# Grouped-query attention on one core: the values' cast moves from a GpSimd instruction to GpSimd's transfers, with a re-made plan of the work

## The chip, the cores and the metric

The kernel runs on one core of one Trainium2 chip. The metric is the device time of one execution in microseconds. A core has a matrix engine (PE in the profile, with its weight loads as PEld), a vector engine (DVE), a scalar engine (ACT), a general engine (POOL, also called GpSimd), and a queue engine (SP) that here only issues transfers. Each engine runs its own instructions in order; semaphores tie them to one another. Transfers (DMAs) can be issued by SP, by ACT and by POOL.

## The reference

Eight batches, eight query heads, two key and value heads, 1024 positions, head size 64, all in float32. Four query heads share one key and value head. For each of the 64 query heads the kernel must compute

```
scores = scale * matmul(q, k.T)          # 1024 x 1024, scale = 1 / 8
attn   = exp(scores - max(scores))
attn   = attn / (sum(attn) + 1e-08)
out    = matmul(attn, v)                 # 1024 x 64
```

## The kernel before, in words

**Jobs and pairs.** Each query head is a job j, 0 to 63 (NJ = 64). A job's scores are computed turned, keys on the partitions, as eight *pairs* of two 128x512 blocks. A pair fills one of three PSUM slots (`sp0` to `sp2`), written by two matmuls (L864), and it is then turned into exponentials in one of two ways.

**The ACT way.** One ACTIVATE over 128x1024 (L874) writes bf16 exponentials into a `pt` tile. PE multiplies them with the values: eight matmuls a pair.

**The DVE way.** One TENSOR_SCALAR, the *first pass* (L885, `dpass`), scales the scores and writes them as 16-bit integers into `yt`, which read as bf16 are nearly powers of two. Two pairs form a *chain*. Over a chain DVE runs two masking instructions on 2048 columns, `zh` (L892) for the mantissa part and `two` (L899) for the exponent part, and a product (L908, `mul`), in place in `zt`. Then PE adds both parts, `et` and `zt`, by matmuls of their own, sixteen a pair. Only for the last four jobs does DVE add them (L913).

**GpSimd's share.** Part of a chain's product is computed by GpSimd (L835, `gmul`), some columns at a time, each while DVE runs a first pass (and the normalization behind it, if there is one). Such a stretch is called a window. The planner works out how many columns fit a window from M_GFIX (fixed ns) and M_GCOL (ns a column), in steps of 32 columns and at least 192. A chain is given up to two windows before DVE does the rest, and only chains that begin with heads 2 to 58 take part.

**Values.** The values of a group (four jobs) stand in one of four `va` tiles of 128 x 4 x 2 x 65 bf16; the 65th number is 1, so the matmuls (L926) also sum the exponentials. SP loads them as float32 into `vs` (L656), and GpSimd casts them into `va` with one instruction (L659, `place_v`). For groups 1 to 15 the planner has an event of its own, `gplace` (L215 to L219): the cast takes 614 ns of a window, and a product follows in the same window only if at least 192 columns still fit.

**Queries and keys.** They are cast to bf16 by transfers that GpSimd issues, from DRAM to DRAM (L623 for one or two heads, L632 for the last head), and turned into SBUF by transposing transfers that SP issues (L667, L677). A cast is due 18 us (q) or 19 us (k) before its first scores and a transpose 11 or 12.5 us. Once GpSimd has had its first product, a cast that is due stands in a list (`casts`). It is issued behind a product when the next product's planned start leaves 650 ns (M_ISSUE, L843); if it gets 5 us late it is issued at once, behind the newest score matmul.

**Output.** A group of up to seven 128-row pieces is finished by a RECIPROCAL (L991, `rec`) and a multiplication (L1000, `norm`) on DVE, then stored by SP (L1004).

**The order.** All of this is laid out by `Plan` when the kernel is built. It steps through a model of PE, ACT and DVE with the M_ constants as durations. At each choice of PE (a score pair for ACT or DVE, a piece of the value matmuls, a dummy matmul, waiting) it looks HORIZON ns ahead, and takes the choice with the least idle time of ACT and DVE, weighted by W_A and W_D (and PE's waste by W_P). `quota` (L151) caps how many of a job's eight pairs go to DVE: FIRST for the first jobs, then MXD, and one more in each MORE-th job. M_BACK caps DVE's backlog when a pair is given to it, M_SPARE says how near the next first pass must be for DVE to leave a chain's product to GpSimd, M_HOLD how long a normalization may wait. The resulting list of events is the order in which each engine gets its instructions.

Of the kernel before, what the change touches and what calls it, by code (L numbers as in the profile page):

```python
# [17 lines left out]
M_FILL = 1e9  # L18
M_IDLE = 350
M_DUMMY = 110  # L20
# [16 lines left out]
M_GLEAD = 160  # L37
M_GFIX = 120
M_GCOL = 2.09
M_GOVER = 60  # L40
M_GLATE = 900
M_NORM = 531
M_HOLD = 2500
M_SPARE = 500
M_ISSUE = 650

M_GAP = 90
M_RUNWAY = 1800
M_BACK = 3000
M_WAIT = 250  # L50
M_TOL = 300

HORIZON = 5500
W_A = 1.0
W_D = .28
W_P = 0
W_LAG = 0
# [4 lines left out]
MXD = 2  # L62
MORE = 6
TAIL = 4
CHN = 2
LONG = 6
FIRST = (2, 1)
GWINS = 2
# [66 lines left out]
class Plan:  # L135
# [5 lines left out]
    def __init__(self, nj, npt, nct, nyt):  # L141
# [32 lines left out]
        s.firstp, s.fleft, s.twice = [INF] * 8, 8, []  # L174
        s.placed = 0
        s.end = False
# [31 lines left out]

    def gpsimd(self, s, t, j, window):

# [3 lines left out]
        at += M_GLEAD  # L214
        g = s.placed + 1  # L215
        if 4 * g - 1 <= j < self.nj and 4 * g < self.nj and at + 614 <= until:
            s.placed = g
            s.note(t, "gplace", None, g, None)
            at = s.tG = at + 614  # L219
        for ch in s.chains:  # L220
# [19 lines left out]
    def dve(self, s):  # L240
# [4 lines left out]
        if rec:  # L245
            _, _, lo, hi = s.norms[0]
            if soon:
                self.gpsimd(s, t, s.dq[0][2], M_REC + 1134 + M_NORM)
                s.host = True
# [4 lines left out]
        elif s.dq and s.dq[0][0] <= t and not (norm and t - s.norms[0][0] > M_HOLD):  # L254
# [15 lines left out]
            if not s.host:  # L270
                self.gpsimd(s, t, j, 1134 + (M_NORM if norm else 0))
            s.host = False
# [271 lines left out]
def kernel(  # L544
# [37 lines left out]
    qp = ctx.enter_context(tc.tile_pool(name="qp", bufs=8))  # L582
    vsp = ctx.enter_context(tc.tile_pool(name="vsp", bufs=2))
    pp = ctx.enter_context(tc.tile_pool(name="pp", bufs=NPT))
# [43 lines left out]
    def cast_q(j):  # L628
        b, h = divmod(j, H)
        if j == NJ - 1:  # L630
            t = qd[j] = dram.tile([HS, 2 * D], BF16, name=f"qd{j}")
            return nc.gpsimd.dma_start(  # L632
                out=t.rearrange("(c p) d -> p c d", p=128), in_=rows(q[b, h], True)
            )
        n = 2 if j > 2 else 1
        t = dram.tile([n * HS, 2 * D], BF16, name=f"qd{j}")
        for i in range(n):
            qd[j + i] = t[i * HS : (i + 1) * HS, :]
        return cast(q.rearrange("b h s d -> (b h s) d")[j * S : (j + n) * S, :], t)
# [13 lines left out]
    def load_v(b, g):  # L653
        t = vsp.tile([128, NH, 2 * D], FP32, name="vs")
        vs[(b, g)] = t
        return nc.sync.dma_start(out=t, in_=rows(v[b, g], b == g == 0))  # L656

    def place_v(b, g):
        return nc.gpsimd.tensor_copy(  # L659
            out=va[(b * G + g) % NVA][:, :, :, 0:D],  # L660
            in_=vs.pop((b, g)).rearrange("p c (two d) -> p c two d", two=2),
        )

# [16 lines left out]
    need, pvs, done = {}, {}, {}  # L680
    places = {}
    for t, kind, x, j, *_ in plan.ev:
        if kind == "score":
            need.setdefault(j, t)
        if kind == "pv":
            pvs.setdefault(x // NPIECE, t)
        if kind == "gplace":
            places[j] = t

# [72 lines left out]
    for j in range(NJ):  # L762
# [15 lines left out]
    for x in [e for e in plan.ev if e[1] == "norm"]:  # L778
# [28 lines left out]

    begun = [e for e in ev if e[1] in ("gmul", "gplace")]
    starts = [e[0] + M_GLEAD for e in begun] + [INF]
# [4 lines left out]
    def begin(kind, j, gate):  # L814
        ins = cast_k(*j) if kind == "ck" else cast_q(j)
        if now and gate:
            tc.add_manual_dep(ins.ins, now.ins.name, Sync, reason="loads in time, not sooner")

    for when, kind, x, j, c, *cols in ev:
        if casts and casts[0][0] < when - 5000:  # L820
            begin(*casts.pop(0)[1:], True)
        if kind in ("ck", "cq"):
# [5 lines left out]
        elif kind in ("gmul", "gplace"):  # L828

            if kind == "gplace":  # L830
                gps = place_v(*divmod(j, G))
            else:
                lo, w = c
                z = flat(zt[j])[:, lo : lo + w]
                gps = nc.gpsimd.tensor_tensor(  # L835
                    out=z, in0=flat(yt[j])[:, lo : lo + w], in1=z, op=ALU.mult
                )
# [12 lines left out]
        elif kind == "tq":  # L850
            turn_q(j)
        elif kind == "lv":
            load_v(*j)
        elif kind == "pl":
# [184 lines left out]
```

## Time and profile before

| | |
|---|---|
| median of 3 runs | 358.98 us (358.1 to 359.25) |
| the profiled execution | 358.87 us, its span 357.0 us |
| granted TensorE clock | 0.998 |
| busy: PE, DVE, ACT, POOL | 345.1, 347.9, 347.3, 149.8 us |
| first exponentials on ACT, last end on ACT | 6.19 us, 351.5 us |
| ACT exponentials (L874) | 374, 344.8 us busy |
| DVE first passes (L885) | 138, 167.6 us busy |
| GpSimd products (L835) | 98, 113.7 us busy |
| GpSimd casts of values (L659) | 16, 10.2 us busy |
| GpSimd issues of q and k casts (L623, L632) | 41, 27.2 us |
| DMA engines, mean share by queue | 41.9% (SP's), 19.3% (GpSimd's) |

The busy time of a group is the time in which at least one of its instructions ran; the mean duration beside it in the lines below is that of one instruction with its tail. Two DVE instructions in a row overlap by about 0.08 us, and ACT's by about 0.12 us, so the time from one start to the next is shorter than the mean. A POOL line with DMA_DIRECT2D is the time GpSimd takes to issue a transfer, not the time of the transfer.

### The profile page before, as it was taken

The page shows a single profiled execution, that of the slowest core. Times are in us where ns is not written, and L with a number is a line of the kernel's source. Part 1 is how long each engine was busy: PE and PEld are TensorE (multiplying, and loading weights), DVE is VectorE, ACT ScalarE, POOL GpSimd, SP SyncE. Part 2 cuts the span into 40 slices and gives each one's busy share as a digit, 9 for nine tenths or more (in the row PEclk, how much of TensorE's full clock was granted, in tenths as well). Part 3 has the DMA queues.
Part 4 walks back from the last instruction along what each step waited for, and adds up shares of the span by engine and source line. Part 5 has one row for each costly group of instructions (what it writes and reads, how often), then busy time and mean ns, then how long its engine had stood idle before and what let it go on. Part 6 is the DMA issues. An engine that isn't in the chain of part 4 may idle for free.

```text
span 357.0 us, 13990 instructions
## 1 busy us (share of the span) xinstructions
PE 345.1 (97%) x6196; PEld 221.2 (62%) x6196; DVE 347.9 (97%) x512; ACT 347.3 (97%) x378; POOL 149.8 (42%) x161
## 2 busy tenths in 40 slices
PE   7899999999999999999999999999999999999995
PEld 3456566666666666666666666666666666666764
DVE  5999999999999999999999999999999999999995
ACT  5999999999999999999999999999999999999993
POOL 3015465654547455345454445222464543531000
PEclk9999999999999999999999999999999999999999
DMA  7937748657646686478655775666854865734323
GB/s 176 118 76 120 150 93 190 146 98 161 137 105 106 157 140 148 80 146 166 121 119 130 126 150 125 130 131 107 146 133 99 161 155 101 147 83 87 77 62 120
DMA packets 88221, 44.82 MB, mean 126 GB/s; under 512 B 45408, under 2 KB 87008, under 8 KB 87520
## 3 DMA queue, kind: packets, MB, share of 16 engines
q1 hardware_dynamic: 86208, 33.44, 41.9%
q0 software_dynamic: 1808, 10.23, 19.3%
q8 instruction: 48, 0.79, 0.9%
q10 hardware_dynamic: 144, 0.26, 0.2%
q14 instruction: 13, 0.11, 0.1%
HBM read 25.17 MB, written 27.00 MB: 146 GB/s over the span
## 4 chain that ended last, share of the span: by engine, by line
ACT 49%; PE 28%; DVE 18%; DMA 2%; issue 2%; DVEq 0%; POOLq 0%
ACT pt L874 49%; PE ops L926 15%; PE sp L864 12%; DVE yt L885 9%; DVE zt L908 3%; DVE et L899 2%; DVE ost L1000 2%; DVE zt L892 1%; DMA qt<-qd 1%; DMA qd<-in_q_dram 1%; PE sp L966 1%; DVE rec L991 1%; DVEq L899 0%; POOLq L1023 0%
## 5 line engine op out<-in xcount | busy, mean ns | idle before, releaser
L874 ACT ACTIVATE pt<-sp 128x1024 bf16<-128x1024 f32 x374 | 344.8, 1041 | 0.8 <-PE sp L864 0.5
L864 PE MATMUL sp<-qt,kt 64*128 64x512 bf16 x1024 | 172.6, 382 | 5.7 <-DVE yt L885 1.6
L926 PE MATMUL ops<-va,pt 128*128 128x65 bf16 x2904 | 175.3, 194 | 0.0
L885 DVE TENSOR_SCALAR yt<-sp 128x1024 uint16<-128x1024 f32 x138 | 167.6, 1214 | 1.0 <-PE sp L864 1.0
L835 POOL TENSOR_TENSOR zt<-yt,zt 128x416 bf16<-128x416 bf16 (+3 forms) x98 | 113.7, 1160 | 111.3 <-DVE et L899 52.8
L926 PEld LDWEIGHTS <-pt 128*128 128x128 bf16 x2904 | 128.3, 97 | 32.5 <-issue 32.5
L926 PE MATMUL ops<-va,zt 128*128 128x65 bf16 x1064 | 126.1, 194 | 0.6 <-DVE zt L908 0.6
L926 PE MATMUL ops<-va,et 128*128 128x65 bf16 x1016 | 117.5, 194 | 0.0
L926 PEld LDWEIGHTS <-zt 128*128 128x128 bf16 x1064 | 84.9, 97 | 14.4 <-issue 13.5
L926 PEld LDWEIGHTS <-et 128*128 128x128 bf16 x1016 | 80.1, 98 | 21.7 <-issue 21.7
L864 PEld LDWEIGHTS <-kt 64*128 64x128 bf16 x1024 | 48.1, 93 | 56.4 <-issue 33.9
L908 DVE TENSOR_TENSOR zt<-yt,zt 128x960 bf16<-128x960 bf16 (+7 forms) x70 | 56.4, 807 | 0.0
L892 DVE TENSOR_SCALAR zt<-yt 128x2048 uint16<-128x2048 uint16 (+1 forms) x70 | 47.6, 680 | 0.3
L899 DVE TENSOR_SCALAR et<-yt 128x2048 uint16<-128x2048 uint16 (+1 forms) x70 | 46.7, 673 | 0.0
L1000 DVE TENSOR_TENSOR ost<-ops,rec 128x448 f32<-128x448 f32 (+2 forms) x73 | 44.3, 606 | 0.2
L623 POOL DMA_DIRECT2D qd<-in_q_dram x32 | 21.1, 658 | 20.2 <-PE sp L864 19.4
L659 POOL CAST va<-vs 128x512 bf16<-128x512 f32 x16 | 10.2, 635 | 34.0 <-DVE ost L1000 15.6
L991 DVE RECIPROCAL rec<-ops 128x7 f32<-128x7 f32 (+2 forms) x73 | 14.1, 194 | 0.0
L623 POOL DMA_DIRECT2D kd<-in_k_dram x8 | 5.3, 666 | 6.9 <-PE ops L926 4.9
L713 PE MATMUL ops<-warm 128*128 128x128 bf16 (+1 forms) x28 | 5.5, 318 | 1.2 <-DVE warm L617 1.2
L913 DVE TENSOR_TENSOR zt<-et,zt 128x2048 bf16<-128x2048 bf16 (+1 forms) x5 | 5.5, 1100 | 0.0
L713 PEld LDWEIGHTS <-warm 128*128 128x128 bf16 x28 | 2.3, 112 | 3.9 <-issue 2.8
(37 smaller groups left out, 23.4 us busy)
## 6 DMA issues: line engine op xcount, KB each, us to landing
out_dram<-ost SPq DMA_DIRECT2D x64, 256.0 KB, 3.2
qd<-in_q_dram POOLq DMA_DIRECT2D x30, 256.0 KB, 4.6
vs<-in_v_dram SPq DMA_DIRECT2D x16, 256.0 KB, 3.8
kt<-kt SPq DMA_DIRECT2D x30, 64.0 KB, 2.8
kd<-in_k_dram POOLq DMA_DIRECT2D x7, 256.0 KB, 5.0
qt<-qd SPq DMA_TRANSPOSE x63, 3.8
qd<-in_q_dram POOLq DMA_DIRECT2D x3, 128.0 KB, 4.0
q<-in_q_dram ACTq DMA_DIRECT2D x1, 256.0 KB, 3.4
```

The costliest lines, as they stand in the source:

```text
L623: return nc.gpsimd.dma_start(out=t.rearrange("(a x) d -> a (x d)", a=128), in_=src.rearrange("(a x) d -> a (x d)", a=128),)
L659: return nc.gpsimd.tensor_copy(out=va[(b * G + g) % NVA][:, :, :, 0:D], in_=vs.pop((b, g)).rearrange("p c (two d) -> p c two d", two=2),)
L835: gps = nc.gpsimd.tensor_tensor(out=z, in0=flat(yt[j])[:, lo : lo + w], in1=z, op=ALU.mult)
L864: now = nc.tensor.matmul(sps[x][:, half, :], lhsT=t[lo : lo + D, c // NH, ci % NH * 128 : (ci % NH + 1) * 128], rhs=qt[j][lo : lo + D, 0, ...
L874: exps.append(nc.scalar.activation(out=p, in_=where_s[(j, c)], func=AF.Exp, scale=scale))
L885: vec = nc.vector.tensor_scalar(out=yt[ch][:, i, :, :], in0=where_s[c], scalar1=EXP_A, scalar2=EXP_B, op0=ALU.mult, op1=ALU.add,)
L892: vec = nc.vector.tensor_scalar(out=zt[j][:, 0:c], in0=yt[j][:, 0:c], scalar1=0x7F, scalar2=0x3F00, op0=ALU.bitwise_and, op1=ALU.bitwise_or,)
L899: vec = ins = nc.vector.tensor_scalar(out=et[j][:, 0:c], in0=yt[j][:, 0:c], scalar1=0x7F80, scalar2=None, op0=ALU.bitwise_and,)
L908: vec = nc.vector.tensor_tensor(out=z, in0=flat(yt[j])[:, 0 : cols[0]], in1=z, op=ALU.mult)
L926: nc.tensor.matmul(ops[plan.group_of[x] % 2][:, lo : lo + D + 1], lhsT=p[:, qs * 128 : (qs + 1) * 128], rhs=va[(b * G + h // HPG) % NVA][: ...
L991: vec = nc.vector.reciprocal(out=to, in_=sums)
L1000: vec = nc.vector.tensor_tensor(out=to, in0=o, in1=by, op=ALU.mult)
```

## The change

Groups 1 to 15 of the values no longer go through `vs` and a GpSimd instruction. For each group two transfers issued by GpSimd read the float32 values in DRAM and write bf16 straight into `va`, one for the even and one for the odd rows of a pair (`two` = 0 and 1). They are due 12 us before the group's first scores and go through the same list as the other casts. The planner's `gplace` event is gone, and with it `placed`, `places` and the load by SP; group 0 is still loaded by SP and cast by GpSimd. Query casts are grouped otherwise: head 3 alone, heads 4 and 5, ..., 60 and 61 in twos, 62 and 63 alone; the first casts and transposes get due times just behind the first scores, where they were before them. The planner's constants change, and so its list of events.

```
-M_IDLE = 350
+M_IDLE = 250
-M_GFIX = 120
-M_GCOL = 2.09
+M_GFIX = 190
+M_GCOL = 1.88
-M_HOLD = 2500
-M_SPARE = 500
+M_HOLD = 1500
+M_SPARE = 800
-M_RUNWAY = 1800
-M_BACK = 3000
+M_RUNWAY = 2100
+M_BACK = 4100
-M_TOL = 300
-HORIZON = 5500
+M_TOL = 200
+HORIZON = 7000
-W_P = 0
+W_P = 0.02
-MORE = 6
+MORE = 4
-FIRST = (2, 1)
+FIRST = (2, 2, 1)
...
-        g = s.placed + 1
-        if 4 * g - 1 <= j < self.nj and 4 * g < self.nj and at + 614 <= until:
-            s.placed = g
-            s.note(t, "gplace", None, g, None)
-            at = s.tG = at + 614
...
-        n = 2 if j > 2 else 1
+        n = 2 if 3 < j < NJ - 2 else 1
...
+    def cast_v(b, g, two):
+        return nc.gpsimd.dma_start(
+            out=va[(b * G + g) % NVA][:, :, two, 0:D],
+            in_=v[b, g].rearrange("(c p two) d -> p c two d", p=128, two=2)[:, :, two, :],
+        )
...
-                ev.append((at - 19000, "ck", None, (b, g), None))
+                ev.append((max(at - 19000, M_START + 200), "ck", None, (b, g), None))
...
-            ev.append((places[j // HPG] - 8000, "lv", None, (b, g), None))
+            for two in range(2):
+                ev.append((at - 12000, "cv", None, (b, g, two), None))
...
-        if j > 2 and (j % 2 or j == NJ - 1):
-            ev.append((at - 18000, "cq", None, j, None))
+        if j == 3 or (j > 3 and j % 2 == 0) or j == NJ - 1:
+            ev.append((max(at - 18000, M_START + 100), "cq", None, j, None))
         if j > 1:
-            ev.append((at - 11000, "tq", None, j, None))
+            ev.append((max(at - 11000, M_START + 100 * j), "tq", None, j, None))
...
-            took = 614 if kind == "gplace" else M_GFIX + M_GCOL * c[1]
+            took = M_GFIX + M_GCOL * w
```

More of the change, by code (lines that the diff above doesn't have):

```diff
@@ L42 @@
 M_NORM = 531
-M_HOLD = 2500
-M_SPARE = 500
+M_HOLD = 1500
+M_SPARE = 800
 M_ISSUE = 650
 M_GAP = 90
-M_RUNWAY = 1800
-M_BACK = 3000
+M_RUNWAY = 2100
+M_BACK = 4100
 M_WAIT = 250
-M_TOL = 300
-HORIZON = 5500
+M_TOL = 200
+HORIZON = 7000
 W_A = 1.0
-W_D = .28
-W_P = 0
+W_D = 0.28
+W_P = 0.02
 W_LAG = 0
@@ L174, in __init__ @@
         s.firstp, s.fleft, s.twice = [INF] * 8, 8, []
-        s.placed = 0
         s.end = False
@@ L207, in act, with gpsimd @@
             self.ready(s, j, c, s.slot[sl])
-    def gpsimd(self, s, t, j, window):
+    def gpsimd(self, s, t, window):
         at = max(t, s.tG)
@@ L247, in dve @@
             if soon:
-                self.gpsimd(s, t, s.dq[0][2], M_REC + 1134 + M_NORM)
+                self.gpsimd(s, t, M_REC + 1134 + M_NORM)
                 s.host = True
@@ L270, in dve @@
             if not s.host:
-                self.gpsimd(s, t, j, 1134 + (M_NORM if norm else 0))
+                self.gpsimd(s, t, 1134 + (M_NORM if norm else 0))
             s.host = False
@@ L582 @@
     qp = ctx.enter_context(tc.tile_pool(name="qp", bufs=8))
-    vsp = ctx.enter_context(tc.tile_pool(name="vsp", bufs=2))
+    vsp = ctx.enter_context(tc.tile_pool(name="vsp", bufs=1))
     pp = ctx.enter_context(tc.tile_pool(name="pp", bufs=NPT))
@@ L655, in load_v @@
         vs[(b, g)] = t
-        return nc.sync.dma_start(out=t, in_=rows(v[b, g], b == g == 0))
+        return nc.sync.dma_start(out=t, in_=rows(v[b, g], True))
     def place_v(b, g):
@@ L680 @@
     need, pvs, done = {}, {}, {}
-    places = {}
     for t, kind, x, j, *_ in plan.ev:
@@ L686 @@
             pvs.setdefault(x // NPIECE, t)
-        if kind == "gplace":
-            places[j] = t
     f32 = {x: kvp.tile([128, NH, 2 * D], FP32, name=f"{x}32") for x in "kq"}
@@ L806, in terms @@
                 yield ci, pt[(j, c)][:, par, :]
-    begun = [e for e in ev if e[1] in ("gmul", "gplace")]
+    begun = [e for e in ev if e[1] == "gmul"]
     starts = [e[0] + M_GLEAD for e in begun] + [INF]
@@ L814, in begin @@
     def begin(kind, j, gate):
-        ins = cast_k(*j) if kind == "ck" else cast_q(j)
+        ins = cast_q(j) if kind == "cq" else (cast_k if kind == "ck" else cast_v)(*j)
         if now and gate:
@@ L821 @@
             begin(*casts.pop(0)[1:], True)
-        if kind in ("ck", "cq"):
+        if kind in ("ck", "cq", "cv"):
             if gps is None:
@@ L827 @@
                 casts.append((when, kind, j))
[L828 to L837, printed above, removed]
+        elif kind == "gmul":
+            lo, w = c
+            z = flat(zt[j])[:, lo : lo + w]
+            gps = nc.gpsimd.tensor_tensor(
+                out=z, in0=flat(yt[j])[:, lo : lo + w], in1=z, op=ALU.mult
+            )
             tc.add_manual_dep(gps.ins, vec.ins.name, Sync, reason="VectorE needs the port before")
-            took = 614 if kind == "gplace" else M_GFIX + M_GCOL * c[1]
+            took = M_GFIX + M_GCOL * w
             free = max(free, when + M_GLEAD) + took
@@ L851 @@
             turn_q(j)
-        elif kind == "lv":
-            load_v(*j)
         elif kind == "pl":
```

## The prediction

> **What bounds the kernel now.** I read the busy shares first, then the stretches, then the groups of instructions by form, then single passages of the timeline. The busy shares alone leave three candidates:
>
> ```profile
> PE 345.1 (97%) x6196; PEld 221.2 (62%) x6196; DVE 347.9 (97%) x512; ACT 347.3 (97%) x378; POOL 149.8 (42%) x161
> ```
>
> The stretches from the middle of the run (columns: us, then PE, PEld, DVE, ACT and POOL, each with its number of instructions, clock, DMA share, GB/s):
>
> ```profile
> 80.00:120.00 40.00, 39.84 (x730) 25.71 (x728) 40.00 (x62) 40.00 (x45) 21.92 (x22) 1.00 0.63 124
> 200.00:240.00 40.00, 39.82 (x733) 25.95 (x732) 39.93 (x58) 40.00 (x45) 15.59 (x17) 1.00 0.60 121
> 280.00:320.00 40.00, 39.77 (x716) 25.41 (x713) 39.90 (x58) 40.00 (x44) 18.09 (x18) 1.00 0.62 130
> ```
>
> DVE and ACT have no hole at all; the clock is full. PE's share is one of overlapping matmuls and is no bound. So the end moves only if both ACT and DVE get less to do. POOL has time, but only between and beside DVE's instructions. The groups by form give the prices:
>
> ```profile
> L874 ACT ACTIVATE pt<-sp 128x1024 bf16<-128x1024 f32 x374 | 344.8, 1041 | 0.8 <-PE sp L864 0.5
> L885 DVE TENSOR_SCALAR yt<-sp 128x1024 uint16<-128x1024 f32 x138 | 167.6, 1214 | 1.0 <-PE sp L864 1.0
> L835 POOL TENSOR_TENSOR zt<-yt,zt 128x416 bf16<-128x416 bf16 x56 | 54.6, 974 | 56.3 <-DVE et L899 21.6 <-DVE zt L892 16.2 <-PE sp L864 5.4
> L835 POOL TENSOR_TENSOR zt<-yt,zt 128x672 bf16<-128x672 bf16 x35 | 50.9, 1455 | 47.8 <-DVE et L899 30.5 <-DVE zt L892 9.0 <-DVE zt L908 4.3
> L908 DVE TENSOR_TENSOR zt<-yt,zt 128x960 bf16<-128x960 bf16 x30 | 18.9, 630 | 0.0
> L908 DVE TENSOR_TENSOR zt<-yt,zt 128x2048 bf16<-128x2048 bf16 x13 | 15.6, 1201 | 0.0
> L659 POOL CAST va<-vs 128x512 bf16<-128x512 f32 x16 | 10.2, 635 | 34.0 <-DVE ost L1000 15.6 <-DMA vs<-in_v_dram 7.9 <-DVE zt L908 4.3
> L632 POOL DMA_DIRECT2D qd<-in_q_dram x1 | 0.8, 808 | 4.4 <-PE sp L864 4.4
> ```
>
> An ACT exponential costs 344.8 / 374 = 0.922 us. GpSimd's product costs (1455 - 974) / 256 = 1.88 ns a column and 974 - 416 x 1.88 = 192 ns fixed; DVE's costs (1201 - 630) / 1088 = 0.525 ns a column. DVE instructions overlap their neighbours by some 0.08 us, so I price them from start to start:
>
> ```profile
> 44.03 1.22 DVE L885 TENSOR_SCALAR yt<-sp 128x1024 uint16<-128x1024 f32 x1
> 45.16 0.68 DVE L899 TENSOR_SCALAR et<-yt 128x2048 uint16<-128x2048 uint16 x1
> 45.76 1.22 DVE L885 TENSOR_SCALAR yt<-sp 128x1024 uint16<-128x1024 f32 x1
> ```
> ```profile
> 44.19 0.97 POOL L835 TENSOR_TENSOR zt<-yt,zt 128x416 bf16<-128x416 bf16 x1 [1.38 <-DVE zt L892]
> 45.10 0.84 POOL L623 DMA_DIRECT2D qd<-in_q_dram  x1
> 45.96 0.98 POOL L835 TENSOR_TENSOR zt<-yt,zt 128x416 bf16<-128x416 bf16 x1
> ```
>
> A first pass is 1.13 us, a masking instruction (L892 or L899) over two pairs 0.60 us. The product runs inside the window of the first pass; a cast issued behind it lasts 0.84 us here, until 0.10 us after the masking ends (45.16 + 0.68 = 45.84; 45.94), and the next product starts at once behind it, 0.20 us after its pass instead of 0.16.
>
> **The change, part by part.**
>
> *The split of the pairs.* Quotas worked out by hand: before 2 + 1 + 62 x 2 + 11 = 138 for DVE, which is the x138 above; after 2 + 2 + 1 + 61 x 2 + 15 = 142. If all are taken, ACT gives up 4 x 0.922 = 3.7 us. A pair on DVE costs 1.13 (first pass) + 0.60 (half of two maskings) + 0.03 (half of the product's fixed part) + 1024 x 0.525 = 0.54 (its product): 2.30 us, so four cost 9.2 us. The eight matmuls more per pair on PE (32 in all, about 0.03 us apart in the timeline, 1 us) lie in PE's holes; without that cover they would cost that 1 us.
>
> *What GpSimd takes off DVE.* By the groups GpSimd multiplied 56 x 416 + 35 x 672 + 3 x 704 + 4 x 384 = 50,464 columns in 98 instructions. With the new constants a window of one first pass (1134 + 60 - 160 - 190 = 844 ns) holds 844 / 1.88 = 448 columns instead of 416; with a normalization behind it, 704 instead of 672. The new constants are the trace's own (192 and 1.88), so the plan errs less, but the product now ends 0.06 us after the window. That costs nothing by the timeline: products ending up to 0.11 us into DVE's next instruction left its interval at 0.60. How many windows are used is not to be seen. Low end: 98 again, 38 of them wide as now: 38 x 704 + 60 x 448 = 53,632. High end: two windows for each of 63 eligible chains (127 pairs of heads 2 to 58), 49 wide: 49 x 704 + 77 x 448 = 68,992. Of the 14 casts in that stretch, four shared their window with a 384-column product, so ten windows come free; three more pairs give three; some 16 passes have neither, and the larger backlog (M_BACK 4100) and the longer reservation (M_SPARE 800) may fill six. I take 98 + 10 + 3 + 6 = 117, nearer to the high end since the ten are certain: 45 x 704 + 72 x 448 = 63,936, which is 13,472 more, or 7.1 us less on DVE (ends 1.7 and 9.7).
>
> *The sum of the two.* With four pairs moved, DVE would have 9.2 - 7.1 = 2.1 us too much, so the planner, whose quota is only a ceiling, should move fewer: n pairs where -0.922 n = 2.30 n - 7.1, n = 2.2, and both engines get 2.0 us less (ends: 0.5 and 2.8). **Term: -2.0 us.**
>
> *The casts of the values.* Removed: 15 POOL casts of about 0.61 to 0.64 us and 15 SP loads (256 KB, 3.8 us to landing, never waited for by PE). Added: 30 POOL issues, two a group, each of 128 x 4 runs of 64 numbers, and two single-head q casts (35 instead of 33, since head 3 and head 62 go alone). POOL's sum, 30 x 0.81 - 15 x 0.63 = +15 us on 150, is no bound. What counts is the queue: behind each issue stands the next product, and behind that, on the port, DVE. The nearest row for 512 runs is L632, 0.81 us; a q cast beside a DVE product takes 0.55. Beside a DVE product of 0.6 us or more both fit the gap: free. Behind a single masking, as at 45.10, a q cast already fills it: 12 of the 34 issues after the first product stand so in the timeline, 11 of 30 by that share. There the extra is between 0 (the descriptors are made while the port is held) and 0.81 - 0.55 = 0.26 us (made only afterwards). I take the middle, 0.13, since neither is seen: the product then ends 0.06 + 0.13 into DVE's next instruction, 0.08 past the 0.11 that cost nothing; 11 x 0.08 = 0.9, and about half of the windows are followed by a reciprocal (0.11 us) that hides it. **Term: +0.5 us**; ends 0 and 30 x 0.25 = 7.5. The removed casts gain nothing beyond the windows already counted.
>
> The Trainium skill (SBUF — State Buffer, A bandwidth-pool intuition that's wrong) says that a transfer issued by GpSimd waits for a DVE instruction that holds the shared port until about 115 ns after its end; the 0.10 us above agrees, and it speaks against putting 30 more of them here. The skill (DMA: Bandwidth & Descriptors, Anatomy of one DMA) also calls descriptor generation small, with many before the cost shows; L632 against the q cast (0.81, 0.55) differs. By that page the term would be 0 and the sum -2.3.
>
> *The transfers.* L632's transfer moved 512 packets of 256 B in 3.2 us from issue to landing. Due 12 us, at most 5 us late, before the group's first scores, with PV later still, the values are in time by 3 us or more; if they were not, PE would wait at L926, where it does not now. Its packets took 27.1% of 16 engines over 5 us, so thirty such take 0.11 of the span, on a DMA share of 0.60 to 0.63; the removed loads give part back. SP loses 15 issues that stood between stores and transposes; nobody waits for SP, so 0 (a loss is excluded: nothing is added to SP).
>
> *The start.* Head 3's cast alone behind the first scores, instead of heads 3 and 4 at 2.9 us. Between 9.5 and 10.2 us PE waits 0.7 us for head 1's transpose, and then DVE:
>
> ```profile
> 10.59 1.22 DVE L885 TENSOR_SCALAR yt<-sp 128x1024 uint16<-128x1024 f32 x1 [0.52 <-PE sp L864]
> ```
>
> With less in front of it the transpose lands earlier; between 0 and 0.5 us, and ACT is not idle there, so it only helps DVE's side. **Term: -0.3 us.** Head 3 is due near 22 us; issued near 7, it lands by 12 and is turned by 17: nothing late.
>
> *The other constants* (M_HOLD, M_RUNWAY, M_TOL, M_IDLE, HORIZON, W_P) only reorder. DVE's recorded idle time is 1.0 us at L885 and ACT's 0.8 at L874, so at most about 1 us is there to win, or a similar amount to lose; I take 0.
>
> Sum: -2.0 + 0.5 - 0.3 = -1.8 us. The profiled execution took 358.87 (span 357.0 and 1.87 around it), 0.11 below the median of 358.98. Forecast: 358.98 - 1.8 = **357.2 us**.
>
> **The rivals.**
> 1. *GpSimd's issues stall DVE (slower).* Place: products behind a value cast and a masking. Price: the full 0.26 late, 0.25 of it on DVE. The gain of 2.3 is eaten at 9 such stalls; from 14 it is measurably slower; at 18 of 30, 4.5 - 2.3 = +2.2: 361.2. For it: 12 issues so placed now, product right behind. Against: 22 of 34 cost nothing.
> 2. *DVE becomes the bound.* All 142 are taken with 117 windows: +2.1 - 0.3 = +1.8, 360.8; with 98 windows, 9.2 - 1.7 - 0.3 = +7.2, 366.2. For it: all 138 were taken before. Against: the plan counts DVE's time itself.
> 3. *No real change:* the freed windows stay unused and the split moves nothing, -0.5 and +0.5 of casts: 358.7 to 359.0.
> 4. *ACT's full gain:* nearly all 126 windows, no stalls: -3.7 - 0.3, 355.0.
>
> **How the numbers follow.** Forecast 0.38, rival 4 0.08, rival 3 0.18, rival 1 0.22, rival 2 0.14. A difference within 0.3% (1.1 us) is about what a measurement can't tell from none. Faster 0.46, same 0.18, slower 0.36. The range reaches from rival 4's edge (355.0) to beyond rival 2's first price: 355.0 to 361.8, leaving out the upper parts of rivals 1 and 2. The forecast's own range is 356.2 to 357.9.
>
> **What would show it.** Right: L874 between x370 and x372, L885 x140 to x142, over 110 products at L835 in sizes 448 and 704, DVE without holes, value issues of about 0.8 us beside products and 0.9 to 1.0 behind maskings. Wrong: L835 still near 50,000 columns; L892 and L899 well over 0.70 us in the mean (stalls at the port); ACT with idle time behind PE; PE waiting at L926 for the value casts.

## The result, and the profile after

The changed kernel takes 359.86 us (median of 17 runs, 358.68 to 361.34), the kernel before on the same chip 358.10 us (17 runs, 357.08 to 360.25). The ratio is 1.0045 with a 95% interval of 1.0028 to 1.0062: slower by 0.45%, some 1.6 us. The forecast was 357.2 us, 1.8 us less than the 358.98 of the three runs known then; the time went the other way. It lies inside the range of 355.0 to 361.8, on the side of the first rival. The profiled execution of the changed kernel took 360.52 us (span 358.7).

First the busy shares and the stretches of the changed kernel (columns as before: us, then PE, PEld, DVE, ACT and POOL with their instructions, clock, DMA share, GB/s):

```profile
PE 346.6 (97%) x6236; PEld 222.4 (62%) x6236; DVE 348.4 (97%) x516; ACT 346.3 (97%) x376; POOL 182.9 (51%) x186
```
```profile
80.00:120.00 40.00, 39.40 (x716) 25.31 (x712) 40.00 (x60) 39.88 (x44) 20.91 (x23) 1.00 0.89 131
200.00:240.00 40.00, 39.01 (x708) 24.68 (x705) 39.93 (x59) 39.59 (x43) 22.53 (x22) 1.00 0.70 118
280.00:320.00 40.00, 39.86 (x728) 25.81 (x725) 40.00 (x61) 40.00 (x44) 23.48 (x22) 1.00 0.66 117
```

DVE is still full. ACT, which had no hole in these stretches before, has one now, 0.41 us between 200 and 240 us, and PE's there grew from 0.18 to 0.99. DVE's fullness is worth a second thought, since an instruction that GpSimd's work holds up counts as busy: a masking of 1.52 us instead of 0.68 stands below. The groups by form (busy us, mean ns, then the idle time in front and who ended it):

```profile
L866 ACT ACTIVATE pt<-sp 128x1024 bf16<-128x1024 f32 x372 | 343.8, 1036 | 1.9 <-PE sp L856 1.5
L877 DVE TENSOR_SCALAR yt<-sp 128x1024 uint16<-128x1024 f32 x140 | 169.3, 1209 | 0.8 <-PE sp L856 0.8
L829 POOL TENSOR_TENSOR zt<-yt,zt 128x448 bf16<-128x448 bf16 x63 | 65.6, 1041 | 58.8 <-DVE zt L884 24.9 <-DVE et L891 11.1 <-PE ops L918 8.5
L829 POOL TENSOR_TENSOR zt<-yt,zt 128x704 bf16<-128x704 bf16 x36 | 54.7, 1518 | 54.9 <-DVE et L891 37.5 <-DVE zt L884 12.1 <-PE sp L856 4.8
L829 POOL TENSOR_TENSOR zt<-yt,zt 128x768 bf16<-128x768 bf16 x7 | 11.5, 1637 | 18.7 <-DVE rec L983 18.7
L884 DVE TENSOR_SCALAR zt<-yt 128x2048 uint16<-128x2048 uint16 x69 | 47.9, 694 | 0.2
L659 POOL DMA_DIRECT2D va<-in_v_dram x30 | 25.7, 858 | 3.1 <-PE sp L856 2.4
```

The split moved as forecast: 372 exponentials on ACT, 140 first passes on DVE. (In the changed file L856 is the score matmul, L866 ACT's exponential, L877 the first pass, L884 and L891 the maskings, L900 DVE's product, L829 GpSimd's, L659 the values' cast, L918 the value matmuls.) GpSimd's products are 63 x 448 + 36 x 704 + 7 x 768 + one of 416 = 59,360 columns in 107 instructions: 8,896 more than before, not 13,472. And ACT's idle time in front of its exponentials has grown from 0.8 to 1.9 us, 1.5 of it behind PE (before 0.5). Whom PE waited for, by the table of waits (us in total, times, longest), before and after:

```profile
PE sp L864 <- DVE yt L885: 1.6, 7, 0.3
```
```profile
PE sp L856 <- DVE yt L877: 3.4, 11, 0.7
```

So DVE frees a score slot late, PE writes the next scores late, and ACT gets them late. No wait for the transfers of the values stands in PE's table.

**Where the 1.7 us of span came from.** I sum DVE's intervals from one start to the next, from its first first pass to its last instruction, and price each at what its kind and size takes where nothing disturbs it (a first pass 1.134 us, a masking over 2048 columns 0.60, a product 0.063 + 0.5235 ns a column, and so on). The rest is excess. All of this is worked out from the two timelines:

| us | before | after | difference |
|---|---|---|---|
| first first pass starts | 6.41 | 6.90 | +0.49 |
| DVE's instructions at undisturbed prices | 342.92 | 341.72 | -1.20 |
| excess of the intervals | 3.75 | 5.36 | +1.61 |
| last DVE start to the end of the span | 3.93 | 4.76 | +0.83 |
| span | 357.00 | 358.74 | +1.74 |

The 0.49 us of the first row go with the moment at which PE's clock became full in the two profiled executions (last section); it differs by as much among kernels that share the start of after.

So the plan did take work off DVE: 1.2 us, of which 1.1 is one addition (L905) of 2048 columns less among the last heads. Off ACT too: two exponentials, 1.84 us; but its first exponential starts 0.28 us later, and the excess of ACT's intervals over 0.917 us rose from 2.21 to 3.81, so ACT's last exponential ends at 351.54 instead of 351.53. Nothing of the gain reached the end. In DVE's excess of 5.36, nine instructions held by a GpSimd product that started late behind a value cast make 2.72, and five maskings lengthened beside a value cast 0.87. (The expectations below say seven and 2.4: they leave out two of 0.15 each, at 36.43 and 187.14, that have a query cast beside them; but there too a late product runs 0.26 us into the masking.) The cost of a late product is regular: in all nine DVE's instruction is longer by the time for which the product runs into it, less 0.12 us (0.26 and 0.15 at 36.43, 0.96 and 0.84 at 168.39). The costliest place, in three views of the timeline (start, us, engine and instruction). First POOL:

```profile
164.65 1.64 POOL L829 TENSOR_TENSOR zt<-yt,zt 128x768 bf16<-128x768 bf16 x1 [4.88 <-DVE rec L983]
166.23 1.67 POOL L659 DMA_DIRECT2D va<-in_v_dram  x2
167.91 1.44 POOL L829 TENSOR_TENSOR zt<-yt,zt 128x448 bf16<-128x448 bf16 x1
```

DVE at the same time:

```profile
166.13 0.70 DVE L891 TENSOR_SCALAR et<-yt 128x2048 uint16<-128x2048 uint16 x1
166.76 1.21 DVE L877 TENSOR_SCALAR yt<-sp 128x1024 uint16<-128x1024 f32 x1
167.89 0.58 DVE L900 TENSOR_TENSOR zt<-yt,zt 128x832 bf16<-128x832 bf16 x1
168.39 1.52 DVE L884 TENSOR_SCALAR zt<-yt 128x2048 uint16<-128x2048 uint16 x1
169.83 1.21 DVE L877 TENSOR_SCALAR yt<-sp 128x1024 uint16<-128x1024 f32 x1
```

And then PE and ACT:

```profile
171.09 0.61 PE L856 MATMUL sp<-qt,kt 64*128 64x512 bf16 x4 [0.66 <-DVE yt L877]
```
```profile
171.74 1.02 ACT L866 ACTIVATE pt<-sp 128x1024 bf16<-128x1024 f32 x1 [0.24 <-PE sp L856]
```

Read it from the top. Both halves of a group's values are issued in one gap and take 1.67 us, from 166.23 to 167.90. The product meant for the first pass at 166.76 starts at 167.91, when that pass is over. It runs beside DVE's product, takes 1.44 us there instead of 1.04, ends at 169.35, and DVE's masking, started at 168.39, lasts 1.52 us instead of 0.68. The next first pass is 0.84 us late, PE's scores wait 0.66, ACT 0.24.

### The profile page after: what moved, and what is told of

Same layout as the page of the kernel before. It is cut to its first block, busy times and chain, and to the rows that moved or that the text cites. A ratio compares the mean times of both kernels' runs of the same rounds, so it can differ in the third digit from the quotient of the medians.

```text
span 358.7 us, 14051 instructions
## 1 busy us (share of the span) xinstructions
PE 346.6 (97%) x6236; PEld 222.4 (62%) x6236; DVE 348.4 (97%) x516; ACT 346.3 (97%) x376; POOL 182.9 (51%) x186
## 3 DMA queue, kind: packets, MB, share of 16 engines
q0 software_dynamic: 17680, 12.19, 31.3%
## 4 chain that ended last, share of the span: by engine, by line
ACT 37%; DVE 34%; PE 24%; issue 3%; DMA 1%; SPq 0%
ACT pt L866 37%; DVE yt L877 18%; PE ops L918 12%; PE sp L856 10%; DVE zt L900 4%; DVE et L891 4%; DVE ost L992 4%; DVE zt L884 3%; DMA kt<-kt 1%; PE ops L710 1%; DVE rec L983 1%; PE sp L958 1%; PE sp L733 0%; PE ops L745 0%; SPq L671 0%
## 5 line engine op out<-in xcount | busy, mean ns | idle before, releaser
L866 ACT ACTIVATE pt<-sp 128x1024 bf16<-128x1024 f32 x372 | 343.8, 1036 | 1.9 <-PE sp L856 1.5
L829 POOL TENSOR_TENSOR zt<-yt,zt 128x448 bf16<-128x448 bf16 (+2 forms) x107 | 132.7, 1240 | 132.4 <-DVE et L891 48.6
L856 PE MATMUL sp<-qt,kt 64*128 64x512 bf16 x1024 | 172.7, 383 | 5.6 <-DVE yt L877 3.4
L918 PE MATMUL ops<-va,pt 128*128 128x65 bf16 x2872 | 175.4, 194 | 0.0
L877 DVE TENSOR_SCALAR yt<-sp 128x1024 uint16<-128x1024 f32 x140 | 169.3, 1209 | 0.8 <-PE sp L856 0.8
L918 PEld LDWEIGHTS <-pt 128*128 128x128 bf16 x2872 | 127.8, 97 | 34.2 <-issue 34.2
L918 PE MATMUL ops<-va,zt 128*128 128x65 bf16 x1096 | 127.6, 194 | 0.0
L918 PE MATMUL ops<-va,et 128*128 128x65 bf16 x1048 | 117.9, 194 | 0.0
L918 PEld LDWEIGHTS <-zt 128*128 128x128 bf16 x1096 | 87.4, 97 | 14.6 <-issue 14.0
L918 PEld LDWEIGHTS <-et 128*128 128x128 bf16 x1048 | 82.3, 98 | 17.7 <-issue 17.7
L856 PEld LDWEIGHTS <-kt 64*128 64x128 bf16 x1024 | 47.8, 93 | 58.0 <-issue 36.4
L900 DVE TENSOR_TENSOR zt<-yt,zt 128x896 bf16<-128x896 bf16 (+9 forms) x71 | 55.0, 775 | 0.0
L884 DVE TENSOR_SCALAR zt<-yt 128x2048 uint16<-128x2048 uint16 (+1 forms) x71 | 48.6, 685 | 0.2
L891 DVE TENSOR_SCALAR et<-yt 128x2048 uint16<-128x2048 uint16 (+1 forms) x71 | 47.7, 677 | 0.0
L659 POOL DMA_DIRECT2D va<-in_v_dram x30 | 25.7, 858 | 3.1 <-PE sp L856 2.4
```

The lines of the kernel that those rows point to most:

```text
L659: return nc.gpsimd.dma_start(out=va[(b * G + g) % NVA][:, :, two, 0:D], in_=v[b, g].rearrange("(c p two) d -> p c two d", p=128, two=2)[:, ...
L829: gps = nc.gpsimd.tensor_tensor(out=z, in0=flat(yt[j])[:, lo : lo + w], in1=z, op=ALU.mult)
L856: now = nc.tensor.matmul(sps[x][:, half, :], lhsT=t[lo : lo + D, c // NH, ci % NH * 128 : (ci % NH + 1) * 128], rhs=qt[j][lo : lo + D, 0, ...
L866: exps.append(nc.scalar.activation(out=p, in_=where_s[(j, c)], func=AF.Exp, scale=scale))
L877: vec = nc.vector.tensor_scalar(out=yt[ch][:, i, :, :], in0=where_s[c], scalar1=EXP_A, scalar2=EXP_B, op0=ALU.mult, op1=ALU.add,)
L884: vec = nc.vector.tensor_scalar(out=zt[j][:, 0:c], in0=yt[j][:, 0:c], scalar1=0x7F, scalar2=0x3F00, op0=ALU.bitwise_and, op1=ALU.bitwise_or,)
```

## The experiments

Theory one: the time went into the issues of the value casts, which push GpSimd's products out of their windows. The rivals: the new constants made a plan that its own model misjudges; the start; the end. Each ratio is to the kernel before, on the same chip. "After" below is the changed kernel.

**24 of the 30 value casts left out.**

```
-            for two in range(2):
+            for two in range(2) if j < 4 * HPG else ():
```

> The changed kernel without 24 of its 30 value issues: groups 4 to 15 multiply with the values of an earlier group that still stand in their tile, so that part of the output is left out; the order of everything else on PE, ACT and DVE is the same. Theory 1 (the value issues of GpSimd push the next product out of its window and that product holds DVE's next instruction): the seven products that are late behind a value issue and the five maskings lengthened beside one (2.4 and 0.9 us of DVE's chain in the profile) fall to one or two, PE waits less for DVE, and the time falls from 359.9 by 2.0 to 2.8 us, to 357.1 to 357.9, at or below the kernel before. Theory 2 (the new order of the work itself is the slower one, however the values arrive): within 0.4 us of 359.9.

Measured: 357.19 us, ratio 0.9982 (0.9970 to 0.9993). DVE's excess falls from 5.36 to 2.90, its undisturbed sum is the same 341.72, and PE waits for DVE's first passes 1.3 us instead of 3.4. Products late behind the six casts that are left: two, 0.58 us. So the 24 casts cost the difference of 1.0045 and 0.9982, some 2.3 us; the plan without them is worth only some 0.6.

**A value cast counted at 950 ns instead of 650.**

```
-            while casts and starts[nth] > free + M_ISSUE:
+            while casts and starts[nth] > free + (M_VISSUE if casts[0][1] == "cv" else M_ISSUE):
+                free += M_VISSUE if casts[0][1] == "cv" else M_ISSUE
                 begin(*casts.pop(0)[1:], False)
-                free += M_ISSUE
```

> The changed kernel, with a value issue counted as 950 ns instead of 650 when the place behind a product is chosen (the q and k casts stay at 650). PE, ACT and DVE keep their order. Theory 1: a pair of value issues no longer goes into a gap of 1.3 us, late products behind value issues fall from seven to three or fewer, time 357.8 to 358.9. Theory 2: 359.5 to 360.2. A third possibility: casts find no place, come 5 us late and are forced in wherever the order stands; then late products stay or grow, and the time is 359.9 or above.

Measured: 359.94 us, 1.0059 (1.0046 to 1.0072): no better, as the third possibility has it. By the kernel's own list, nine value casts now find no gap for 5 us and are then issued at once, wherever that is. Seven products are late, 2.61 us, where nine and 2.72 were, and the place at 168 us is as it was. There is too little room of that size; a right price alone does not help.

**The changed kernel with the constants of before** (all thirteen, FIRST and MORE among them):

```
-M_GFIX = 190
-M_GCOL = 1.88
+M_GFIX = 120
+M_GCOL = 2.09
...
-MORE = 4
+MORE = 6
...
-FIRST = (2, 2, 1)
+FIRST = (2, 1)
```

> The changed kernel with all thirteen planner constants of the kernel before (374 pairs on ACT and 138 on DVE again): the transfers of the values and the new grouping of the q casts alone. Theory 1: it has the stalls behind value issues, about 3 us of late products from 25 us on, against 1.1 us of stalls beside the old casts that it loses, and gets nothing on ACT: 359.5 to 361. Theory 2: 357.5 to 358.5, like the kernel before or a little better, since the constants are then to blame.

Measured: 360.69 us, 1.0086 (1.0073 to 1.0099), slower than after. 374 exponentials and 138 first passes again, 101 products with 51,616 columns; DVE's undisturbed sum is 342.31 and its excess 6.59. The time is as expected, the stalls are others: no product right behind a value cast costs DVE more than 0.1 us. Three maskings beside a value cast are 0.09 and three 0.20 to 0.21 longer, and the second product behind the pair of casts at 182.63 runs 1.24 us into a masking, which takes 1.80 us. So the new constants aren't what costs the time; they give some back. The opposite combination, the old casts in the new plan, was not tried.

**Values cast to DRAM, as the keys are.** Eight casts, all but the first of two groups, in long runs, and SP's queue brings the bf16 values into `va`, two transfers a group.

```
+    def cast_v(b, g):
+        n = G - g
+        t = dram.tile([n * HS, 2 * D], BF16, name=f"vd{b}_{g}")
+        for i in range(n):
+            vd[(b, g + i)] = t[i * HS : (i + 1) * HS, :]
+        lo = (b * G + g) * S
+        return cast(v.rearrange("b g s d -> (b g s) d")[lo : lo + n * S, :], t)
+
+    def put_v(b, g):
+        src = vd[(b, g)].rearrange("(c p) (two d) -> p c two d", p=128, two=2)
+        for two in range(2):
+            nc.sync.dma_start(out=va[(b * G + g) % NVA][:, :, two, 0:D], in_=src[:, :, two, :])
```

> The changed kernel with the values cast like the keys: one GpSimd issue for two groups casts from DRAM to DRAM (8 issues of about 0.55 to 0.85 us instead of 30 of 0.86), and SP then loads the bf16 values into their place with two transfers a group. The whole output is computed. PE, ACT and DVE keep their order. Theory 1: nearly as good as without the value issues, 357.3 to 358.1. Theory 2: 359.5 to 360.2. If SP's 30 more issues matter, transposes come late and PE waits for a transfer; then above 360.

Measured: 357.54 us, 0.9991 (0.9981 to 1.0001). DVE's excess is 2.94; two products late behind a query cast, 0.73, none behind a value cast. ACT's last exponential ends at 349.14, 2.4 us earlier than after.

**The two halves of a group apart**, due 14 and 9 us ahead:

```
-                ev.append((at - 12000, "cv", None, (b, g, two), None))
+                ev.append((at - 14000 + 5000 * two, "cv", None, (b, g, two), None))
```

> The changed kernel with a group's two value issues due 5 us apart (14 and 9 us before the group's first scores) instead of together; everything else as in the changed kernel. If most of the loss comes from two issues of 0.8 us in one gap counted as 1.3 us, the largest jumps (0.84 us at 168, 0.42 at 57 and at 230) go and the time falls by 1.0 to 1.8 us against the changed kernel (ratio to the kernel before 1.000 to 1.002). If each issue behind a masking costs by itself, the sum stays near 3 us, with more and smaller jumps: ratio 1.003 to 1.006.

Measured: 358.96 us, 1.0018 (1.0002 to 1.0034), between after and the two without the issues. The place at 166 us, POOL and then DVE:

```profile
165.50 0.91 POOL L659 DMA_DIRECT2D va<-in_v_dram  x1
166.43 1.05 POOL L829 TENSOR_TENSOR zt<-yt,zt 128x448 bf16<-128x448 bf16 x1
```
```profile
166.02 1.21 DVE L877 TENSOR_SCALAR yt<-sp 128x1024 uint16<-128x1024 f32 x1
167.15 0.79 DVE L900 TENSOR_TENSOR zt<-yt,zt 128x832 bf16<-128x832 bf16 x1
```

One cast alone ends at 166.41, 0.31 us behind the masking (165.39 + 0.71 = 166.10); the product ends at 167.48, 0.25 us behind the first pass, and DVE's product is longer by 0.21 (0.79 against 0.58). The 0.84 is gone; but instead of nine late products there are twelve, eleven of 0.15 to 0.21 us and one of 0.53, and their sum is nearly the same, 2.64 against 2.72. What fell are the maskings lengthened beside a value cast, from 0.87 to 0.24 us (two over 0.05). So the time lies where the first answer puts it, and the sum of the late products where the second does: a pair costs more at its place, but a single cast behind a masking already costs 0.2 us, and there are more of them.

**As many casts, in long runs.** The 30 casts at the same due times, each a contiguous half of a group from DRAM to DRAM; SP places them with four transfers a group.

```
+    def cast_v(b, g, part):
+        t = vd[(b, g, part)] = dram.tile([HS // 2, 2 * D], BF16, name=f"vd{b}_{g}_{part}")
+        return cast(v[b, g][part * HS : (part + 1) * HS, :], t)
```

> As many value issues as in the changed kernel (30, due at the same times), but each casts one contiguous half of a group's values from DRAM to DRAM as the q casts do, and SP loads them into their place with four transfers a group; the whole output is computed. If the length of one issue (the 512 short runs: 0.76 us alone, 0.31 us on after the end of a masking instead of 0.10) makes the loss, the issues take 0.49 to 0.55 us and the ratio to the kernel before is 0.999 to 1.001. If it is the number of issues, the ratio stays at 1.003 to 1.005.

Measured: 357.25 us, 0.9983 (0.9964 to 1.0003), as fast as with 24 casts left out. DVE's excess is 2.62. The group of the value casts, and POOL at the same place:

```profile
L617 POOL DMA_DIRECT2D vd<-in_v_dram x30 | 18.9, 630 | 2.4 <-PE sp L864 2.4
```
```profile
163.38 1.64 POOL L835 TENSOR_TENSOR zt<-yt,zt 128x768 bf16<-128x768 bf16 x1 [4.88 <-DVE rec L991]
164.97 1.19 POOL L617 DMA_DIRECT2D vd<-in_v_dram  x2
166.16 1.06 POOL L835 TENSOR_TENSOR zt<-yt,zt 128x448 bf16<-128x448 bf16 x1
```

DVE there:

```profile
165.49 1.21 DVE L885 TENSOR_SCALAR yt<-sp 128x1024 uint16<-128x1024 f32 x1
166.62 1.06 DVE L908 TENSOR_TENSOR zt<-yt,zt 128x832 bf16<-128x832 bf16 x1
167.60 0.68 DVE L892 TENSOR_SCALAR zt<-yt 128x2048 uint16<-128x2048 uint16 x1
```

A pair takes 1.19 us instead of 1.67 and fits the 1.3 that the list counts. Even so this one product costs DVE 0.48 us; no other behind a value cast does. With as many issues at the same due times the loss is gone: it is the length of an issue (630 ns in the mean against 858), not the number, that cost the time. The transfers differ too, in what they move and where to. That PE never waited for either speaks against a part of that in the time; and that the length goes with the runs and not with the place they are written to shows in the last head's query cast, 512 runs from DRAM to DRAM: in this same kernel it takes 0.76 us beside a first pass, where a long-run cast takes 0.49.

**The due times of the first query casts as before**, on top of the values cast to DRAM:

```
-            ev.append((max(at - 18000, M_START + 100), "cq", None, j, None))
+            ev.append((at - 18000, "cq", None, j, None))
-            ev.append((max(at - 11000, M_START + 100 * j), "tq", None, j, None))
+            ev.append((at - 11000, "tq", None, j, None))
```

> The kernel that casts the values to DRAM (ratio 0.9991), with the due times of the first q casts and transposes as in the kernel before: head 3's cast goes out at once, before the first scores. In the four kernels profiled with the new constants DVE's first pass began at 6.75 to 6.90 us, in the two with the old ones at 6.35 and 6.41; the first query block landed at 3.7 to 3.85 against 4.0 and 4.2, and PE's first 128-column matmuls lasted 0.31 us against 0.22. If head 3's early cast delays that block until PE is at full speed, the first pass returns to 6.4 and the time falls by 0.3 to 0.5 us. If the first pass is a matter of the run, it differs from run to run whatever the order, and the time stays within 0.2 us; if the early cast delays head 1's transpose again, DVE waits 0.5 us near 10 us as in the kernel before.

Measured: 357.73 us, 1.0009 (0.9982 to 1.0036), not to be told from 0.9991; nine of the twelve runs took 357.0 to 358.2 us, three 360.8 to 361.3, and no run shows why. Its first first pass starts at 6.75 us, late as in after, and with the due times of after it starts at 6.40 in the kernel with the halves apart: the due times didn't delay it. Nor does the wait for head 1's transpose come back: from the second first pass to the third it is 1.87 us, as in after, and 2.47 in the kernel before.

**Query casts in fours** from head 8 on, 21 issues instead of 34, on top of the values cast to DRAM:

```
+    def heads_of(j):
+        return 4 if 8 <= j < NJ - 4 else 2 if 3 < j < NJ - 2 else 1
```

> The kernel that casts the values to DRAM (ratio 0.9991), with the q casts of heads 8 to 59 in fours instead of twos (21 issues instead of 35, due 20 us ahead instead of 18). If GpSimd's remaining issues still cost (two products late behind a q cast, 0.7 us of DVE), the time falls by 0.3 to 0.8 us: ratio 0.997 to 0.9985. If the larger transfers crowd out transposes and stores, PE waits for a transfer at the scores and the ratio is above 1.

Measured: 357.72 us, 0.9992 (0.9971 to 1.0012): nothing gained. One late product instead of two (0.42 and not 0.73).

**Another quota for the last heads**, on top of the values cast to DRAM. In the plan of after, PE is still at head 62's value matmuls when ACT is done; the new quotas give the late heads other shares.

```
-TAIL = 4
+TAIL = 5
...
+        for j, n in ((54, 4), (55, 1), (59, 3), (60, 3), (62, 0)):
+            self.quota[j] = n
```

> The kernel that casts the values to DRAM (ratio 0.9991), with DVE's pairs shared out otherwise at the end: quotas of heads 54, 55, 59, 60 and 62 are 4, 1, 3, 3 and 0 instead of 3, 2, 2, 2 and 3, and DVE itself adds the parts of the last five heads instead of four (TAIL 5). In the kernels with the new constants DVE ended 3.0 to 3.1 us after the last exponential, against 2.2 us in the kernel before, since PE was still at the matmuls of head 62 when the last exponentials came. If the new plan lost its gain in that tail, DVE now ends 2.0 us or less after the last exponential and the time falls by 0.5 to 1.0 us: ratio 0.996 to 0.998. If the tail is set by something else, the ratio stays at 0.999.

Measured: 356.25 us, 0.9947 (0.9929 to 0.9966), faster than both kernels, and by more than the first answer had it. 373 exponentials, 139 first passes, 109 products with 60,320 columns. The last instructions of DVE, first in after, then in this kernel:

```profile
353.74 0.21 DVE L983 RECIPROCAL rec<-sp 128x8 f32<-128x8 f32 x1 [0.99 <-PE sp L958]
353.98 0.69 DVE L992 TENSOR_TENSOR ost<-sp,rec 128x512 f32<-128x512 f32 x1
```
```profile
350.54 0.21 DVE L995 RECIPROCAL rec<-sp 128x8 f32<-128x8 f32 x1 [1.25 <-PE sp L970]
350.79 0.69 DVE L1004 TENSOR_TENSOR ost<-sp,rec 128x512 f32<-128x512 f32 x1
```

ACT's last exponential ended at 351.54 in after and at 350.03 here. From there to DVE's last end it is 3.13 us in after, 3.03 with the values cast to DRAM and the old quotas, 2.23 in the kernel before and 1.45 here. In after PE's last matmuls start only when ACT is through:

```profile
351.54 1.66 PE L958 MATMUL sp<-va,pt 128*128 128x65 bf16 x48
```

In the kernel before, the like matmuls began here:

```profile
350.63 0.67 PE L966 MATMUL sp<-va,pt 128*128 128x65 bf16 x16
```

**The same quotas with the query casts in fours:**

> The same other sharing of DVE's pairs at the end, on the kernel with the q casts in fours (ratio 0.9992). Same reasons and numbers: 0.996 to 0.998 if the tail was the loss; and if fewer q issues help by themselves, 0.2 to 0.4 us below the run with twos.

Measured: 356.20 us, 0.9956 (0.9936 to 0.9975): the same as without the fours.

## Why the prediction was wrong

**The step that failed: "Term: +0.5 us", the casts of the values.** The first rival's mechanism was the right one. By the ratios with 24 casts left out (0.9982) and with 30 long-run casts (0.9983), the casts as written cost 0.0062 of 358, 2.2 us, with some 0.9 of uncertainty either way, where the term had 0.5; DVE's excess differs by 2.5 and 2.7 us. Three things in the term were off, and one held:

- Of the two ends for a cast behind a masking, "made only afterwards" was the true one, and I took the middle. A query cast ends 0.10 us after the masking's end, a value cast some 0.31: 0.21 more, near the upper end of 0.26.
- I counted 30 single casts. Of the 30, 22 go in pairs into one gap: 1.58 to 1.78 us a pair (the first took 2.02) where the list counts 1.3. This wasn't in the text at all, although the diff gives both halves one due time. Five of the nine late products stand behind a pair, 1.97 of the 2.72 us; but parting the pairs made more late products and left the sum as it was.
- The cast itself, not only the product behind it, lengthens a masking that starts while it runs, by 0.15 to 0.21 us: five times, 0.87 in all.
- The price of a late product held: free for 0.11 us, then as long as it lasts. What I had wrong is how far the products run into DVE's next instruction: 0.26 to 0.96 us in the nine, where I took 0.19.

The rival asked for 14 stalls of 0.25 us to be measurably slower. Nine were enough, at 0.30 in the mean, with the five lengthened maskings, since the gain that they had to eat up was smaller than the 2.3 us it reckoned with.

**"Term: -2.0 us", the split and GpSimd's columns.** The number of pairs was right (n = 2; x372, x140). The columns were not: 8,896 more instead of 13,472, which is 4.7 us off DVE instead of 7.1. The two pairs cost 2 x 2.30 = 4.6 us, so the two cancel; that DVE's undisturbed sum fell by 1.2 all the same is the addition less among the last heads, which I had not counted.

What the plan gives without the casts' delay is 0.17 to 0.18%, some 0.6 us, where -2.0 and -0.3 stood; with the 2.2 of the casts that makes the +1.6 measured. The kernel with the long-run casts shows where the rest stayed: its last exponential ends at 348.96, 2.57 us earlier than before, so the gain arrives there nearly as forecast (with the help of the next point). Then DVE's last end is at 351.99, only 1.77 earlier: 0.80 goes in the end of the plan, a place that the prediction didn't look at. The other 0.91 goes between DVE's last end and the end of the span, which is 3.24 us in the kernel before and anything from 2.95 to 4.16 in the others; whether that is more than chance stays open. Another quota for the last heads brought the ratio from 0.9991 to 0.9947, 1.6 us, with some 0.75 either way. The time between the last exponential and DVE's end shrank by 1.58 (3.03 to 1.45), but that the two agree is chance: the last exponential ends 0.88 later there (one more on ACT), so DVE's end is only 0.69 earlier in the profiles, and 0.54 more lies behind it.

**"The removed casts gain nothing beyond the windows already counted": wrong, in the other direction.** Three of the old casts held DVE up, by 0.29, 0.42 and 0.37 us, 1.08 together. The first, on POOL in the kernel before:

```profile
122.87 0.61 POOL L659 CAST va<-vs 128x512 bf16<-128x512 f32 x1 [1.86 <-DMA vs<-in_v_dram]
123.44 0.91 POOL L835 TENSOR_TENSOR zt<-yt,zt 128x384 bf16<-128x384 bf16 x1
```

and on DVE:

```profile
123.93 0.97 DVE L892 TENSOR_SCALAR zt<-yt 128x2048 uint16<-128x2048 uint16 x1
```

The cast waited 1.86 us for its load, its product ended late, and the masking took 0.97 us instead of 0.68. The idle times that I read showed a wait for that load (7.9 us over the group); I took it for harmless. That those 1.08 us went to the total is read from the trace, not shown by a run of its own.

**"The start: -0.3".** The wait of 0.52 us for head 1's transpose went, as forecast: from the second to the third first pass it is 1.87 us instead of 2.47. But with the due times of before, and four query casts out ahead of the first scores where the kernel before has three, it stays away too, so less work in front of the transpose isn't shown to be the reason. And DVE started 0.49 later. Over all profiles here the first first pass starts anywhere from 6.13 to 6.95, and at 6.40 with the halves apart and 6.95 with the long runs, which both keep the start of after; that goes with the clock of the execution (last section), so single profiles can't tell the sum of the two.

**A count.** The query casts after are 34, not 35 as the prediction and an expectation have it; nothing in the sum rests on it.

**"The transfers": right.** GpSimd's queue went from 19.3% to 31.3% of the DMA engines' span, 12.0 points against an estimate of 11, and PE never waited for values. **"DVE becomes the bound": no**, its undisturbed sum fell.

**What would have shown it.** "L892 and L899 well over 0.70 us in the mean" was too blunt a test: the means are 694 and 684 ns after, 688 and 681 before. One stall of 0.84 us moves a mean of 69 by 12 ns, and several stalls stand in DVE's products. "ACT with idle time behind PE" was the test that spoke.

## What to carry to other kernels

Price a transfer that GpSimd issues by the number of runs that its descriptors need and by what stands beside and behind it, above all where several fall due together; if GpSimd's slots are scarce, cast with long runs to DRAM and let a hardware queue do the scattered placing. What it costs is read in the timeline: here a product of GpSimd cost DVE the time for which it ran into DVE's next instruction, less 0.12 us. A plan that saves time in the middle has to be read to its last instruction: here the end gave back 0.8 to 0.9 us, and another quota there brought 1.6. A mean over a group does not show a few long stalls; list the longest intervals instead.

## What the runs showed of the hardware that I had not expected

- **The issue of many short runs.** Beside a first pass a value cast of 512 runs takes 0.76 to 0.79 us to issue, one of 128 long runs 0.49; beside a DVE product 0.82 to 0.83 and 0.54; behind a masking the one ends 0.31 us after it, the other 0.10. The Trainium skill (DMA: Bandwidth & Descriptors, Anatomy of one DMA) calls descriptor generation small, with many before the cost shows; these runs disagree: here it was 0.27 to 0.29 us an issue, and it decided the sign. The skill's 115 ns after a DVE instruction's end (SBUF — State Buffer, A bandwidth-pool intuition that's wrong) agrees with the long-run casts and not with the short-run ones.
- **A product beside a product is a slower one.** Beside a DVE product, GpSimd's 448 columns took 1.44 us instead of 1.04 (at 167.91); the other late products, which ran beside a first pass, took their usual time.
- **The first matmuls.** The six first score matmuls took 0.83 us in the kernel before, 1.32 in after, and 0.82 with the query casts in fours:

```profile
5.75 0.83 PE L864 MATMUL sp<-qt,kt 64*128 64x512 bf16 x6
```
```profile
5.82 1.32 PE L856 MATMUL sp<-qt,kt 64*128 64x512 bf16 x6
```
```profile
5.48 0.82 PE L869 MATMUL sp<-qt,kt 64*128 64x512 bf16 x6
```

That is where the 0.49 us of a later start come from, and the traces show why. The clock column says 1.00 in all three, but it counts the time ahead of the first clock record as full. That record, of full clock, begins at 4.33 us in the kernel before, at 6.88 in after and at 4.51 with the query casts in fours. In after the first four score matmuls take 0.60 to 0.63 us each, those from 7.5 us on 0.37 to 0.39. In the five profiles whose record begins by 4.92 us the six take 0.82 to 0.84 us and the first first pass starts at 6.13 to 6.41; in the seven where it begins between 6.34 and 7.12, the six take 1.02 to 1.46 and the first pass starts at 6.75 to 6.95. Both groups hold kernels with the new constants and the start of after; the two kernels with the old constants are both in the first group, and two profiles can't say whether that is chance. The Trainium skill (TensorE: Matmul & The Clock Gate, Part 1: The HAM clock gate) says that the window of the clock's warm-up runs freely, so that the point of full speed varies from run to run by some 500 ns either way; that it varies with the execution agrees, but here it varied by 2.8 us, from 4.33 to 7.12.
